# A two-layer hybrid decoder on one core: weights laid out by transfer, per-feature parameters laid out as columns

## The chip, the cores and the metric

The kernel runs on one core of a Trainium2 chip (trn2). The metric is device time in microseconds (us) of one execution. The kernel before takes 655.65 us, the median of three runs that lie between 655.14 and 657.24 us. Engines are named as the profile names them: PE is TensorE (PEld its weight loads), DVE is VectorE, ACT is ScalarE, POOL is GpSimd, and SP is the engine that issues most transfers.

## What is computed

The reference is a decoder trunk of two layers over 256 tokens of width 1024, all in float32:

```
for i in range(2):
    h   = rmsnorm(x, norm1_g[i])
    mix = hybrid_mixer(h, w_in[i], cmp_pos[i], cmp_w1[i], cmp_w2[i])     # 16 heads of three kinds
    x   = x + mix @ w_out[i]
    h   = rmsnorm(x, norm2_g[i])
    x   = x + conv_glu_ffn(h, w_up[i], conv_w[i], conv_b[i], w_down[i])  # 2 x 2816 wide, conv of 3 taps
return rmsnorm(x, final_g)
```

The input projection `h @ w_in` has 2615 columns: queries, keys and values of all heads. One kind of head (NSA) also attends to compressed blocks: blocks of 32 tokens of keys and of values get `cmp_pos` added, go through `cmp_w1` (2048 to 128), a GELU and `cmp_w2`. Two kinds of parameter thus enter: large weight matrices (w_in, cmp_w1, w_out, w_up, w_down), and per-feature vectors (the norm gains, conv_w, conv_b, cmp_pos), which multiply or shift one feature for all tokens.

## The kernel before, in words

**Weights.** Every weight tile but `cmp_w1` comes through `weight` (L148): SP issues one transfer from the weight as the caller gave it into a staging tile `st` (five buffers), ACT rounds it to the PE's fast float format into `hl` (L158), and DVE subtracts to get the rounding error (L160), so that each product is made of three matmuls (`mm3`, L207 to L210) with a high and a low part. `hl` has eight buffers, and a buffer comes free when the matmuls that read it are done. A `w_in` tile is two blocks of 128 rows by 336 to 384 columns (L163), so the transfer has two runs of 1.3 to 1.5 KB for each partition; a `w_up` tile has four runs of 1 KB per partition (L909), a `w_out` tile two runs of 2 KB (L803), a `w_down` tile one run of 4 KB (L911). The `cmp_w1` tile (L605) takes a buffer of `hl`, is used as it lands, and has 16 runs of 512 B per partition.

**Parameters.** The engines need a per-feature vector as a column: feature on the partition. Before, each vector is loaded as rows of 128 features (`rows_n`, and three parts of `rows`), turned by a PE transpose, and copied from PSUM to SBUF by DVE; `columns` (L139 to L142) does both steps. There are five such calls: norm1_g first of all (L232), cmp_pos ahead of the compressed heads (L591, into `colp`), and norm2_g with conv_b and the two layers' conv_w in the dilated heads of layer 0 (L820 to L822). The rows of the last four come by six transfers that POOL issues after the first norm (L270 and L126 to L131), among them `w2` (L271) and the mask constants `cb` (L127).

**Order.** Per layer: seven column chunks of `w_in` (`project`, L564 to L569; here A with 384 columns, B with 336, C with 360, then D to G with 384 each), four `st` transfers a chunk, as a generator that yields between groups of matmuls; `fill` interleaves these with the attention of the heads. After chunks A, B and most of C come the compressed heads: DVE copies the turned keys and values into `u2` (L547), adds the position column and makes `raw` (L597), and 64 small matmuls multiply by `cmp_w1` (L609). Then attention, the output projection (`out_part`) and the MLP, 11 blocks of 256 features: `up` and `down`. The order of instructions on each engine is fixed before the run by the framework's planner, which works with its own estimates of durations and may move an instruction ahead of others; `after(...)` pins a few of them behind a named one.

Of the kernel before, what the change touches and what calls it, by code (L numbers as in the profile page):

```python
# [12 lines left out]
F32 = mybir.dt.float32  # L13
# [7 lines left out]
D = 1024  # L21
DEPTH = 2
DFF = 2816
# [10 lines left out]
B_CAUS, B_DIL = 0, 256  # L34
CONSTB_W = B_DIL + 6 * 128
# [35 lines left out]
def trunk(ctx, tc, x, norm1_g, w_in, cmp_pos, cmp_w1, cmp_w2, w_out, norm2_g, w_up, conv_w, conv_b, w_down,  # L71
          final_g, eye, consts_f, consts_b, out):
# [25 lines left out]
    rn = keep.tile([16, 128], F32, name="rows_n")  # L98
# [3 lines left out]
    nc.scalar.dma_start(rn, norm1_g.rearrange("l (f p) -> (l f) p", p=128))  # L102
# [20 lines left out]
    rows = keep.tile([128, 512], F32, name="rows", tag="R", bufs=1)  # L123
    ra, rp_, rc = rows[:60, 0:128], rows[:64, 128:256], [rows[:66, 256 + 128 * i:384 + 128 * i] for i in range(DEPTH)]

    def other_constants():  # L126
        nc.gpsimd.dma_start(cb, consts_b)  # L127
        for a, b, src in ((0, 16, norm2_g), (16, 60, conv_b)):
            nc.gpsimd.dma_start(ra[a:b, :], src.rearrange("l (f p) -> (l f) p", p=128))
        for i in range(DEPTH):  # L130
            nc.gpsimd.dma_start(rc[i], conv_w[i].rearrange("w (f p) -> (w f) p", p=128))  # L131

    cola = keep.tile([128, 76], F32, name="cola")
    colp = keep.tile([128, DEPTH, 2, 16], F32, name="colp")
    colc = keep.tile([128, DEPTH, 66], F32, name="colc")
    gain1 = [cola[:, 8 * i:8 * i + 8] for i in range(DEPTH)]
    gain2 = [cola[:, 16 + 8 * i:24 + 8 * i] for i in range(DEPTH)]
# [74 lines left out]
    for i in range(DEPTH):  # L212

        with ExitStack() as es:
# [9 lines left out]
            if i == 0:  # L224
# [7 lines left out]
                columns(bank("t"), cola[:, 0:16], rn)  # L232

# [29 lines left out]
            def scales():  # L263
# [551 lines left out]


            dense.append(out_part((0, 1), (2, 3), (4,)))
# [56 lines left out]
            dense.append(out_part((5, 6), (7,)))  # L874
# [23 lines left out]
        with ExitStack() as es:  # L898
# [5 lines left out]
            wu = w_up[i].rearrange("(k p) c -> p k c", p=128)  # L904
            hs = {}

            def up(f):
                f0 = f * 256
                wh = [weight(wu[:, 4 * h:4 * h + 4, au * DFF + f0:au * DFF + f0 + 256], 4, 256)  # L909
                      for au in range(2) for h in range(2)]  # L910
                wd = [weight(w_down[i, (2 * f + s) * 128:(2 * f + s + 1) * 128, None, :], 1, 1024) for s in range(2)]  # L911
# [23 lines left out]
                for s in range(2):  # L935
                    cw = [colc[:, i, w * 22 + 2 * f + s:w * 22 + 2 * f + s + 1] for w in range(3)]
                    cw.append(cola[:, 32 + 22 * i + 2 * f + s:33 + 22 * i + 2 * f + s])
# [84 lines left out]
_INS = ['x', 'norm1_g', 'w_in', 'cmp_pos', 'cmp_w1', 'cmp_w2', 'w_out', 'norm2_g', 'w_up', 'conv_w', 'conv_b',  # L1022
        'w_down', 'final_g']
# [19 lines left out]
```

## Time and profile before

| | |
|---|---|
| median of 3 runs | 655.65 us (655.14 to 657.24) |
| the profiled execution | 657.55 us, its span 655.7 us |
| mean granted PE clock | 0.994 |
| PE busy | 636.8 us (97%) |
| DVE, ACT, POOL busy | 532.2, 400.0, 50.0 us |
| transfers | 76532 packets, 107.28 MB, mean 164 GB/s |

The span runs from the first to the last instruction; the execution has 1.85 us around it. Matmuls overlap, so that one of them is longer than the distance between two starts, and "busy" means that at least one is running. "[2.02 <-issue]" behind an instruction says that its engine was idle for 2.02 us before it and what ended the idle time; "issue" is used where the profile names no releaser. The DMA share is the mean busy share of the 16 DMA engines; it can come out a little above 1.

### The profile page before, as it was taken

The numbers are of one execution on the slowest core, as the hardware profiler recorded it, in microseconds if no ns is written. First come the engines' busy times: TensorE is split into PE (matmuls) and PEld (weight loads), VectorE is DVE, ScalarE is ACT, GpSimd is POOL, SyncE is SP. The second block draws the span as 40 slices with busy tenths as digits, with TensorE's granted clock in tenths as the row PEclk, the third lists the DMA queues.
The fourth block names the chain that finished last, engine by engine and source line by source line (L and its number), as shares of the span: only waits on it lengthen the run. The fifth ranks groups of instructions, "written<-read, shape, count | busy, mean of one in ns | idle before, by whom it ended". The sixth has DMA issues, their size and how long they took to land.

```text
span 655.7 us, 10521 instructions
## 1 busy us (share of the span) xinstructions
PE 636.8 (97%) x3699; PEld 543.2 (83%) x3699; DVE 532.2 (81%) x1185; ACT 400.0 (61%) x773; POOL 50.0 (8%) x119
## 2 busy tenths in 40 slices
PE   8989999999999999999999999999999999999995
PEld 7978987768888888888898888867788888888884
DVE  5879998776988888888777799987598888888873
ACT  6656776866655555555475676786675555555533
POOL 0422210001000000000020132000000000000002
PEclk9989999999999999999999999999999999999998
DMA  8983234453676666665457525234457666666501
GB/s 269 273 255 95 81 97 146 129 165 118 184 217 189 191 190 191 193 192 169 131 164 229 145 81 177 61 117 146 144 161 226 192 193 192 193 193 192 192 2 64
DMA packets 76532, 107.28 MB, mean 164 GB/s; under 512 B 3717, under 2 KB 63414, under 8 KB 76480
## 3 DMA queue, kind: packets, MB, share of 16 engines
q1 hardware_dynamic: 75568, 104.77, 52.9%
q0 software_dynamic: 448, 1.05, 0.5%
q10 hardware_dynamic: 464, 0.79, 0.3%
q8 instruction: 29, 0.48, 0.3%
q14 instruction: 23, 0.19, 0.1%
HBM read 105.55 MB, written 1.05 MB: 163 GB/s over the span
## 4 chain that ended last, share of the span: by engine, by line
PE 81%; DVE 11%; ACT 3%; issue 2%; DMA 1%; POOL 1%; SPq 0%; POOLq 0%; ACTq 0%; DVEq 0%
PE bu L924 24%; PE bu L926 13%; PE bn L208 6%; PE bn L209 6%; PE bn L210 6%; PE bd L208 5%; PE bd L209 5%; PE bd L210 5%; DVE hl L160 3%; PE bs L354 2%; PE bt L374 2%; PE bt L343 1%; DVE acc L486 1%; ACT hl L158 1%; PE bo L609 1%
## 5 line engine op out<-in xcount | busy, mean ns | idle before, releaser
L160 DVE TENSOR_TENSOR hl<-st,hl 128x1024 fp32r<-128x1024 f32 (+3 forms) x208 | 232.5, 1121 | 60.7 <-ACT hl L158 59.7
L158 ACT CAST hl<-st 128x1024 fp32r<-128x1024 f32 (+3 forms) x208 | 201.5, 972 | 121.7 <-PE bn L210 43.5
L924 PE MATMUL bu<-ahl,hl 128*128 128x512 f32 x704 | 177.9, 393 | 2.0 <-DVE ahl L196 2.0
L924 PEld LDWEIGHTS bu<-ahl,hl 128*128 128x128 f32 x704 | 127.2, 189 | 25.9 <-DVE ahl L196 2.8
L926 PEld LDWEIGHTS bu<-ahl,hl 128*128 128x128 f32 x704 | 96.7, 190 | 7.2
L926 PE MATMUL bu<-ahl,hl 128*128 128x256 f32 x704 | 99.3, 282 | 0.0
L208 PE MATMUL bd<-hl,ahl 128*128 128x384 f32 (+2 forms) x256 | 92.9, 367 | 0.9 <-DVE xr L813 0.5
L209 PE MATMUL bd<-hl,ahl 128*128 128x384 f32 (+2 forms) x256 | 91.2, 356 | 0.2 <-DVE hl L160 0.2
L210 PE MATMUL bd<-hl,ahl 128*128 128x384 f32 (+2 forms) x256 | 91.3, 357 | 0.0
L208 PE MATMUL bn<-hl,h_hi 128*128 128x512 f32 x176 | 69.0, 392 | 0.1
L209 PE MATMUL bn<-hl,h_hi 128*128 128x512 f32 x176 | 68.8, 391 | 0.0
L210 PE MATMUL bn<-hl,h_lo 128*128 128x512 f32 x176 | 68.5, 389 | 0.0
L929 ACT COPY cross<-bu 128x256 f32<-128x256 f32 x88 | 32.4, 369 | 40.0 <-PE bu L926 39.7
L208 PEld LDWEIGHTS bd<-hl,ahl 128*128 128x128 f32 x256 | 48.2, 189 | 9.8 <-issue 2.2
L209 PEld LDWEIGHTS bd<-hl,ahl 128*128 128x128 f32 x256 | 48.2, 188 | 3.4 <-issue 0.8
L210 PEld LDWEIGHTS bd<-hl,ahl 128*128 128x128 f32 x256 | 48.2, 188 | 3.0 <-issue 0.9
L941 DVE SCALAR_TENSOR_TENSOR c<-a,colc,c 128x255 f32<-128x255 f32 (+1 forms) x88 | 40.1, 482 | 7.5 <-ACT c L939 6.2
L210 PEld LDWEIGHTS bn<-hl,h_lo 128*128 128x128 f32 x176 | 33.0, 188 | 7.3 <-DVE h_lo L954 0.3
L208 PEld LDWEIGHTS bn<-hl,h_hi 128*128 128x128 f32 x176 | 33.1, 188 | 7.1 <-ACT h_hi L953 0.9
L209 PEld LDWEIGHTS bn<-hl,h_hi 128*128 128x128 f32 x176 | 33.1, 188 | 6.0
L939 ACT ACTIVATE c<-a,cola,colc 128x256 f32<-128x256 f32 x44 | 24.1, 595 | 13.5 <-DVE a L933 13.5
L930 DVE TENSOR_TENSOR sa<-bu,cross 128x256 f32<-128x256 f32 x44 | 18.4, 418 | 6.5 <-ACT cross L929 4.4
(243 smaller groups left out, 797.0 us busy)
## 6 DMA issues: line engine op xcount, KB each, us to landing
st<-in_w_up_dram SPq DMA_DIRECT2D x88, 512.0 KB, 4.1
st<-in_w_down_dram SPq DMA_DIRECT2D x44, 512.0 KB, 4.2
st<-in_w_in_dram SPq DMA_DIRECT2D x40, 384.0 KB, 3.9
st<-in_w_out_dram SPq DMA_DIRECT2D x12, 512.0 KB, 3.8
st<-in_w_in_dram SPq DMA_DIRECT2D x8, 360.0 KB, 3.2
st<-in_w_in_dram SPq DMA_DIRECT2D x8, 336.0 KB, 3.4
st<-in_w_out_dram SPq DMA_DIRECT2D x8, 256.0 KB, 2.9
xr<-in_x_dram SPq DMA_DIRECT2D x3, 256.0 KB, 5.2
```

What stands on the lines that cost most here:

```text
L158: S.copy(hv, sv)
L160: V.tensor_sub(lv, sv, hv.bitcast(F32))
L208: PE.matmul(b, ahi, whi, start=first, stop=False)
L209: PE.matmul(b, ahi, wlo, start=False, stop=False)
L210: return PE.matmul(b, alo, whi, start=False, stop=last)
L354: PE.matmul(b[:, o:o + nk], qa, ka, start=True, stop=True)
L924: PE.matmul(o, wa, hhl[k // 4][:, k % 4].rearrange("p z t -> p (z t)"), start=k == 0, stop=False)
L926: PE.matmul(o[:, :L], wl, hhi[k // 4][:, k % 4, :], start=False, stop=k == 7)
L929: S.copy(cross, o[:, L:])
L930: V.tensor_tensor(sums[au][:, s], o[:, :L], cross, op=OP.add)
L939: S.activation(c[:, o:o + 256], a[:, o:o + 256], AF.Identity, bias=cw[3], scale=cw[2])
L941: V.scalar_tensor_tensor(c[:, o + d:o + 256], a[:, o:o + 256 - d], cw[w], c[:, o + d:o + 256], op0=OP.mult, op1=OP.add)
```

## The change

All of it is in how the host hands over the inputs and how they are loaded. `laid_out` rearranges the weights on the host so that each `st` tile, and each `cmp_w1` tile, is one contiguous block with one run per partition (2.6 to 3 KB for `w_in`, 4 KB for `w_up` and the two-row groups of `w_out`, 8 KB for `cmp_w1`); `w_down` was one run before and stays. The number of transfers of weights, their sizes in bytes and their order in the program stay. The gains of norm1 come as a [128, 16] array, loaded by ACT straight into `cola`; all the other vectors come as one [128, 256] array, which POOL loads into `cols` by one transfer. The five transposes and the five copies are gone, and so are the tile `rows` and five of POOL's transfers.

```diff
+PIECES = ((0, 384), (384, 336), (1103, 360), (719, 384), (1463, 384), (1847, 384), (2231, 384))
+W_IN = {c: sum(n for _, n in PIECES[:j]) for j, (c, n) in enumerate(PIECES)}
+GROUPS = ((0, 1), (2, 3), (4,), (5, 6), (7,))
...
-    rn = keep.tile([16, 128], F32, name="rows_n")
+    cola = keep.tile([128, 16], F32, name="cola")
...
-    nc.scalar.dma_start(rn, norm1_g.rearrange("l (f p) -> (l f) p", p=128))
+    nc.scalar.dma_start(cola, gains)
...
-    def other_constants():
-        nc.gpsimd.dma_start(cb, consts_b)
-        for a, b, src in ((0, 16, norm2_g), (16, 60, conv_b)):
-            nc.gpsimd.dma_start(ra[a:b, :], src.rearrange("l (f p) -> (l f) p", p=128))
-        for i in range(DEPTH):
-            nc.gpsimd.dma_start(rc[i], conv_w[i].rearrange("w (f p) -> (w f) p", p=128))
...
+    cols = keep.tile([128, PARAMS_W], F32, name="cols")
...
-    def columns(b, dst, src):
-        n = src.shape[0]
-        PE.transpose(b[:, :n], src, ident[:n, :n])
-        V.tensor_copy(dst, b[:, :n])
+    gain2 = [cols[:, P_N2 + 8 * i:P_N2 + 8 * i + 8] for i in range(DEPTH)]
+    colp = cols[:, P_POS:P_POS + 64].rearrange("p (l c j) -> p l c j", l=DEPTH, c=2)
...
-        nc.sync.dma_start(sv, src)
+        nc.sync.dma_start(st[:, :a * n], src)
...
+    def piece(w, o, p, n):
+
+        return w[o:o + p * n].rearrange("(p n) -> p n", n=n)
+
     def w_in_chunk(i, c0, n, then=(None,) * 4, behind=(None, None)):
-        w = w_in[i].rearrange("(k p) c -> p k c", p=128)
-        return [weight(w[:, 2 * h:2 * h + 2, c0:c0 + n], 2, n, then[h], behind) for h in range(4)]
+        w = piece(w_in[i], W_IN[c0] * D, 4 * 128, 2 * n)
+        return [weight(w[h * 128:(h + 1) * 128], 2, n, then[h], behind) for h in range(4)]
...
-                columns(bank("t"), cola[:, 0:16], rn)
...
-                        nc.gpsimd.dma_start(rp_, cmp_pos.rearrange("l c (j p) d -> (l c j) (p d)", p=2))
-                    nc.gpsimd.dma_start(w2, cmp_w2[i].rearrange("c h d -> h c d"))
+                        nc.gpsimd.dma_start(cols, params)
+                    nc.gpsimd.dma_start(w2, cmp_w2[i].rearrange("h (c d) -> h c d", c=2))
                     if i == 0:
-                        other_constants()
+                        nc.gpsimd.dma_start(cb, consts_b)
...
-                if i == 0:
-                    with after(newest[0].ins):
-                        columns(bank("t"), colp.rearrange("p l c j -> p (l c j)"), rp_)
...
-                    nc.sync.dma_start(w1, cmp_w1[i, c].rearrange("(j p) h -> p j h", p=128))
+                    nc.sync.dma_start(w1.rearrange("p j h -> p (j h)"), cmp_w1[i, c])
...
-                        wh, wl = weight(w_out[i, g[0] * 128:(g[-1] + 1) * 128, n * 512:(n + 1) * 512]
-                                        .rearrange("(k p) c -> p k c", p=128), len(g), 512)
+                        wh, wl = weight(piece(w_out[i], (8 * n + g[0]) * 128 * 512, 128, len(g) * 512), len(g), 512)
...
-            if i == 0:
-                with after(newest[0].ins):
-                    columns(bank("t"), cola[:, 16:76], ra)
-                    for l in range(DEPTH):
-                        columns(bank("t"), colc[:, l, :], rc[l])
...
-                wh = [weight(wu[:, 4 * h:4 * h + 4, au * DFF + f0:au * DFF + f0 + 256], 4, 256)
+                wh = [weight(w_up[i, f, au, h], 4, 256)
                       for au in range(2) for h in range(2)]
...
+def laid_out(a):
+
+    w = a["w_in"].reshape(DEPTH, 4, 2, 128, -1).transpose(0, 1, 3, 2, 4)
+    w_in = np.concatenate([w[..., c:c + n].reshape(DEPTH, -1) for c, n in PIECES], 1)
...
+    w_up = a["w_up"].reshape(DEPTH, 2, 4, 128, 2, DFF // 256, 256).transpose(0, 5, 4, 1, 3, 2, 6)
+    w1 = a["cmp_w1"].reshape(DEPTH, 2, 16, 128, 128).transpose(0, 1, 3, 2, 4)
...
+    columns = lambda z: z.reshape(-1, 128).T
+    gains = columns(a["norm1_g"])
+    params = np.concatenate([columns(a[z]) for z in ("norm2_g", "conv_b", "cmp_pos", "conv_w")], 1)
```

## Rows read from the trace of the kernel before

**Rows 1.** The page's shares of the chain that ended last, by engine.

```profile
PE 81%; DVE 11%; ACT 3%; issue 2%; DMA 1%; POOL 1%; SPq 0%; POOLq 0%; ACTq 0%; DVEq 0%
```

**Rows 2.** Busy time by stretch. Columns: the stretch, its length, busy us and number of instructions of PE, PEld, DVE, ACT and POOL, then the granted PE clock, the DMA share and GB/s.

```profile
20.00:30.00 10.00, 9.19 (x64) 8.70 (x63) 8.11 (x22) 7.01 (x15) 5.12 (x10) 1.00 1.01 309
30.00:40.00 10.00, 8.14 (x51) 7.50 (x49) 8.32 (x28) 5.24 (x11) 0.26 (x1) 1.00 0.99 306
60.00:70.00 10.00, 9.86 (x54) 8.23 (x53) 9.89 (x45) 7.19 (x19) 2.19 (x7) 1.00 0.15 40
170.00:320.00 150.00, 150.00 (x798) 129.52 (x797) 122.21 (x177) 84.69 (x126) 0.00 (x0) 1.00 0.63 188
```

**Rows 3.** What ACT's weight casts waited for, over the whole span (total us, times, longest).

```profile
ACT hl L158 <- DMA st<-in_w_in_dram: 3.8, 4, 2.4
```

**Rows 4.** The first microseconds, instruction by instruction (start, duration, engine, line).

```profile
1.17 0.45 ACTq L102 DMA_DIRECT2D rows_n<-in_norm_g_dram  x1
5.28 0.26 PE L141 MATMUL bt<-ident,rows_n 16*128 16x16 f32 x1 [0.65 <-DMA ident<-in_eye_dram]
6.62 0.47 ACT L195 ACTIVATE ahl<-bt,cola 128x256 fp32r<-128x256 f32 x1 [3.47 <-PE bt L189]
```

**Rows 5.** Transfers by their issuing line: count, KB each, median us from issue to landing.

```profile
rows_n<-in_norm_g_dram ACTq DMA_DIRECT2D x1, 8.0 KB, 3.9
rows<-in_cmp_pos_dram POOLq DMA_DIRECT2D x1, 32.0 KB, 5.9
st<-in_w_up_dram SPq DMA_DIRECT2D x88, 512.0 KB, 4.1
st<-in_w_down_dram SPq DMA_DIRECT2D x44, 512.0 KB, 4.2
```

**Rows 6.** The chain that ended last, around 25 us (start, duration, what), and PE's row at the end of it.

```profile
18.85 5.51 DMA st<-in_w_in_dram
24.44 0.80 ACT hl L158
...
25.64 0.57 DVE qrT L523
...
26.26 0.55 PE L343 MATMUL bt<-ident,PA 128*128 128x128 f32 x3 [0.81 <-DVE qrT L523]
```

**Rows 7.** ACT, DVE and PE ahead of the compressed heads of layer 0.

```profile
36.29 0.84 ACT L158 CAST hl<-st 128x768 fp32r<-128x768 f32 x1 [2.40 <-DMA st<-in_w_in_dram]
...
34.79 0.92 DVE L547 COPY u<-bt 64x64 f32<-64x64 f32 x4
37.16 0.96 DVE L160 TENSOR_TENSOR hl<-st,hl 128x768 fp32r<-128x768 f32 x1 [1.45 <-ACT hl L158]
38.15 0.22 DVE L142 COPY colp<-bt 128x64 f32<-128x64 f32 x1
38.29 0.95 DVE L160 TENSOR_TENSOR hl<-st,hl 128x768 fp32r<-128x768 f32 x1
...
39.49 1.09 DVE L597 TENSOR_TENSOR raw<-u,colp 128x240 f32<-128x240 f32 x2
...
40.16 3.60 PE L609 MATMUL bo<-w,raw 128*32 128x128 f32 x64 [2.02 <-issue]
```

**Rows 8.** POOL's first issue of the parameters, SP's issues of the two `cmp_w1` tiles of layer 0 and of the `w_in` tile behind them, and all packets that moved in two stretches of 4 us, 30 to 34 and 34 to 38.

```profile
20.66 0.79 POOL L270 DMA_DIRECT2D rows<-in_cmp_pos_dram  x1
...
21.13 0.82 SPq L605 DMA_DIRECT2D w<-in_cmp_w_dram  x1
23.29 3.62 SPq L605 DMA_DIRECT2D w<-in_cmp_w_dram  x1
27.01 4.35 SPq L154 DMA_DIRECT2D st<-in_w_in_dram  x1
...
DMA packets 634, 1.18 MB, mean 295 GB/s; under 512 B 25, under 2 KB 159, under 8 KB 634
DMA packets 1019, 1.48 MB, mean 369 GB/s; under 512 B 59, under 2 KB 1014, under 8 KB 1019
```

**Rows 9.** The second half of the compressed-head matmuls of layer 1 (chain row: start, duration; the first half is in rows 10, and the 64 of layer 0 in rows 7), and the stretches of those of layer 0 and of the first half of layer 1 (columns as in rows 2).

```profile
361.42 1.01 PE bo L609 x32
...
40.20:43.70 3.50, 3.50 (x65) 3.16 (x65) 2.42 (x5) 0.83 (x1) 1.59 (x4) 0.52 0.79 234
358.50:359.60 1.10, 1.10 (x33) 0.90 (x33) 1.07 (x3) 0.00 (x0) 0.00 (x0) 1.00 0.59 221
```

**Rows 10.** The same place in layer 1: DVE's order and PE's wait.

```profile
356.84 0.94 DVE L547 COPY u<-bt 64x64 f32<-64x64 f32 x4
357.81 1.08 DVE L597 TENSOR_TENSOR raw<-u,colp 128x240 f32<-128x240 f32 x2
...
358.50 1.08 PE L609 MATMUL bo<-w,raw 128*32 128x128 f32 x32 [0.58 <-issue]
```

**Rows 11.** The transposes of the parameters that stand on the chain in layer 0 (cmp_pos; then norm2_g with conv_b, and conv_w twice).

```profile
35.28 0.20 PE bt L141
113.75 0.20 PE bt L141
114.73 0.06 PE bt L141
115.49 0.21 PE bt L141
```

More of the change, by code (lines that the diff above doesn't have):

```diff
@@ L34 @@
 B_CAUS, B_DIL = 0, 256
+P_N2, P_CB, P_POS, P_CW = 0, 16, 60, 124
+PARAMS_W = P_CW + 132
+PIECES = ((0, 384), (384, 336), (1103, 360), (719, 384), (1463, 384), (1847, 384), (2231, 384))
+W_IN = {c: sum(n for _, n in PIECES[:j]) for j, (c, n) in enumerate(PIECES)}
+GROUPS = ((0, 1), (2, 3), (4,), (5, 6), (7,))
 CONSTB_W = B_DIL + 6 * 128
@@ L70, in trunk @@
 @with_exitstack
-def trunk(ctx, tc, x, norm1_g, w_in, cmp_pos, cmp_w1, cmp_w2, w_out, norm2_g, w_up, conv_w, conv_b, w_down,
-          final_g, eye, consts_f, consts_b, out):
+def trunk(ctx, tc, x, w_in, cmp_w1, cmp_w2, w_out, w_up, w_down, final_g, gains, params, eye, consts_f, consts_b, out):
     nc = tc.nc
@@ L120, in trunk @@
     V.memset(neghalf, -0.5)
-    rows = keep.tile([128, 512], F32, name="rows", tag="R", bufs=1)
-    ra, rp_, rc = rows[:60, 0:128], rows[:64, 128:256], [rows[:66, 256 + 128 * i:384 + 128 * i] for i in range(DEPTH)]
-    def other_constants():
-        nc.gpsimd.dma_start(cb, consts_b)
-        for a, b, src in ((0, 16, norm2_g), (16, 60, conv_b)):
-            nc.gpsimd.dma_start(ra[a:b, :], src.rearrange("l (f p) -> (l f) p", p=128))
-        for i in range(DEPTH):
-            nc.gpsimd.dma_start(rc[i], conv_w[i].rearrange("w (f p) -> (w f) p", p=128))
-    cola = keep.tile([128, 76], F32, name="cola")
-    colp = keep.tile([128, DEPTH, 2, 16], F32, name="colp")
-    colc = keep.tile([128, DEPTH, 66], F32, name="colc")
-    gain1 = [cola[:, 8 * i:8 * i + 8] for i in range(DEPTH)]
-    gain2 = [cola[:, 16 + 8 * i:24 + 8 * i] for i in range(DEPTH)]
-    def columns(b, dst, src):
-        n = src.shape[0]
-        PE.transpose(b[:, :n], src, ident[:n, :n])
-        V.tensor_copy(dst, b[:, :n])
+    cols = keep.tile([128, PARAMS_W], F32, name="cols")
+    gain1 = [cola[:, 8 * i:8 * i + 8] for i in range(DEPTH)]
+    gain2 = [cols[:, P_N2 + 8 * i:P_N2 + 8 * i + 8] for i in range(DEPTH)]
+    colp = cols[:, P_POS:P_POS + 64].rearrange("p (l c j) -> p l c j", l=DEPTH, c=2)
     def after(ins):
@@ L814, in out_part @@
                 yield
-            dense.append(out_part((0, 1), (2, 3), (4,)))
-            if i == 0:
-                with after(newest[0].ins):
-                    columns(bank("t"), cola[:, 16:76], ra)
-                    for l in range(DEPTH):
-                        columns(bank("t"), colc[:, l, :], rc[l])
+            dense.append(out_part(*GROUPS[:3]))
             nm = pj.tile([128, 12], F32, name="nmd")
@@ L873, in trunk @@
             fill()
-            dense.append(out_part((5, 6), (7,)))
+            dense.append(out_part(*GROUPS[3:]))
             fill(3)
@@ L903, in trunk @@
             NF = DFF // 256
-            wu = w_up[i].rearrange("(k p) c -> p k c", p=128)
             hs = {}
             def up(f):
-                f0 = f * 256
-                wh = [weight(wu[:, 4 * h:4 * h + 4, au * DFF + f0:au * DFF + f0 + 256], 4, 256)
+                wh = [weight(w_up[i, f, au, h], 4, 256)
                       for au in range(2) for h in range(2)]
-                wd = [weight(w_down[i, (2 * f + s) * 128:(2 * f + s + 1) * 128, None, :], 1, 1024) for s in range(2)]
+                wd = [weight(w_down[i, (2 * f + s) * 128:(2 * f + s + 1) * 128, :], 1, 1024) for s in range(2)]
                 order = [(au, s, range(8)) for au in range(2) for s in range(2)]
@@ L935, in up @@
                 for s in range(2):
-                    cw = [colc[:, i, w * 22 + 2 * f + s:w * 22 + 2 * f + s + 1] for w in range(3)]
-                    cw.append(cola[:, 32 + 22 * i + 2 * f + s:33 + 22 * i + 2 * f + s])
+                    cw = [cols[:, o + 2 * f + s:o + 2 * f + s + 1]
+                          for o in [P_CW + 66 * i + 22 * w for w in range(3)] + [P_CB + 22 * i]]
                     o = s * 256
@@ L1019, in trunk @@
                 nc.scalar.dma_start(out[0, t * 128:(t + 1) * 128, 512:1024], y[1])
-_INS = ['x', 'norm1_g', 'w_in', 'cmp_pos', 'cmp_w1', 'cmp_w2', 'w_out', 'norm2_g', 'w_up', 'conv_w', 'conv_b',
-        'w_down', 'final_g']
+def laid_out(a):
+    w = a["w_in"].reshape(DEPTH, 4, 2, 128, -1).transpose(0, 1, 3, 2, 4)
+    w_in = np.concatenate([w[..., c:c + n].reshape(DEPTH, -1) for c, n in PIECES], 1)
+    w = a["w_out"].reshape(DEPTH, 8, 128, 2, 512)
+    w_out = np.concatenate([w[:, g[0]:g[-1] + 1, :, n].transpose(0, 2, 1, 3).reshape(DEPTH, -1)
+                            for n in range(2) for g in GROUPS], 1)
+    w_up = a["w_up"].reshape(DEPTH, 2, 4, 128, 2, DFF // 256, 256).transpose(0, 5, 4, 1, 3, 2, 6)
+    w1 = a["cmp_w1"].reshape(DEPTH, 2, 16, 128, 128).transpose(0, 1, 3, 2, 4)
+    w2 = a["cmp_w2"].transpose(0, 2, 1, 3)
+    columns = lambda z: z.reshape(-1, 128).T
+    gains = columns(a["norm1_g"])
+    params = np.concatenate([columns(a[z]) for z in ("norm2_g", "conv_b", "cmp_pos", "conv_w")], 1)
+    return dict(x=a["x"], w_in=w_in, cmp_w1=w1.reshape(DEPTH, 2, 128, -1), cmp_w2=w2.reshape(DEPTH, 128, -1), w_out=w_out,
+                w_up=w_up.reshape(DEPTH, DFF // 256, 2, 2, 128, 1024), w_down=a["w_down"], final_g=a["final_g"],
+                gains=gains, params=params)
 def kernel(**inputs):
@@ L1032 @@
     eye, cf, cb = shape_constants()
-    given = [(n, np.ascontiguousarray(inputs[n])) for n in _INS] + [("eye", eye), ("consts_f", cf),
-                                                                           ("consts_b", cb)]
+    given = [(n, np.ascontiguousarray(a)) for n, a in laid_out(inputs).items()] + [
+        ("eye", eye), ("consts_f", cf), ("consts_b", cb)]
     for name, a in given:
```

## The prediction

> **What bounds the kernel now.** I read the page's chain first. PE holds 81% of it and transfers 1% [rows 1], so a change to transfers can only pay where the PE stands still or does extra work. The busy time by stretch comes next [rows 2]. In the long MLP stretch from 170 to 320 us PE is busy for all 150.00 us while the DMA share is 0.63, so nothing in that stretch waits for weights. Between 20 and 40 us it is the other way round: the DMA share is 1.01 and 0.99, at 309 and 306 GB/s, and PE lacks 0.81 and 1.86 us. The third view is what ACT's weight casts waited for: over the whole span they waited 3.8 us for transfers, four times, 2.4 us at the longest [rows 3]. So the transfers matter in the first 40 us of layer 0 and hardly elsewhere, and I follow the timeline there.
>
> The clearest place is the compressed heads of layer 0. PE stands for 2.02 us before their 64 matmuls, until 40.16 us. These need `raw`, which DVE writes from 39.49 us on (1.09 us for two, so the first is there at about 40.04). DVE was late because ahead of `raw` in its queue stood a weight subtract that had waited 1.45 us for a cast, and that cast had waited 2.40 us for a `w_in` transfer, up to 36.29; then the `colp` copy (38.15) and another subtract (38.29) [rows 7]. The transfer was late because SP's queue was full of `cmp_w1`: the two issues at 21.13 and 23.29 and the next `w_in` issue at 27.01 held SP for 0.82, 3.62 and 4.35 us, and from 30 to 34 us, when `cmp_w1` with its runs of 512 B still came in, the rate was 295 GB/s, against 369 from 34 to 38, when almost all packets were `w_in` runs of 1.5 KB (1014 of 1019 under 2 KB) [rows 8]. And the stop cost more than itself: the 64 matmuls ran at a granted clock of 0.52 and took 3.60 us; in layer 1, behind a wait of 0.58 us, the two halves took 1.08 and 1.01 us, the first at 1.00 [rows 7, 9, 10]. 0.52 is practically the lower of the two levels, 1.2 GHz.
>
> **The change part by part.**
>
> *The start.* The norm1 transpose held PE for 0.26 us, at 5.28, after the identity had landed, and the first transposes of x and ACT's first step at 6.62 came behind it [rows 4]. Without it this moves up by 0.26, if the gains are there at 6.36. As rows they were issued at 1.17 and landed 3.9 us later [rows 4, 5], at 5.07. As columns they are 128 runs of 64 B, for which the trace has no row: if they take the 5.9 us of the cmp_pos transfer [rows 5], they land at 7.07 and the step loses 0.45. I take the nearer row (same queue, same bytes): gain 0.26, between -0.45 and 0.26.
>
> *The stall at 25 us.* PE lacked 0.81 us because a `w_in` tile issued at 18.85 landed after 5.51 us and ACT and DVE steps stood behind its cast [rows 6]. Its runs go from 1.4 to 2.9 KB. Nearest are `w_up` and `w_down`: 1 KB and 4 KB runs of equal bytes land after 4.1 and 4.2 us [rows 5], so longer runs of this size gain little. Gain 0.2, between 0 and 0.81.
>
> *cmp_w1 in one run, cmp_pos without a turn.* The two tiles are 2.10 MB. At 295 GB/s they occupy the engines for 7.1 us, at 369 for 5.7 [rows 8]: what is queued behind them lands 1.4 us earlier, the tile cast at 36.29 at about 34.9. With DVE's order kept, `raw` starts near 39.49 - 1.4 - 0.15 for the missing copy, 37.9, and PE's wait falls to about 0.8 after its own earlier start. But the order need not stay. Before, `raw` had to follow the copy of a transpose; now its column comes from a transfer that takes the place of POOL's issue at 20.66, which landed 5.9 us later [rows 5, 8], nine us ahead of need. In layer 1, where the columns were there already, the planner put `raw` right behind the four copies to `u2`, and PE waited 0.58 [rows 10]. In layer 0 these copies end at 35.71 [rows 7], before PE wants `raw`. So I keep 0.3 us of the wait: gain 1.7, between 0 and 2.02. Next late is then the rope of the indexer keys after chunk C, which stands behind PE's own work and moves with it. The transpose of cmp_pos is 0.20 us of PE on the chain [rows 11]: gain 0.20.
>
> *The clock.* A wait of 0.81 us left it at 1.00 [rows 2, 6], 2.02 us did not. If the wait is under 0.8, the 64 matmuls take 1.08 + 1.01 instead of 3.60 us: gain 1.5, between 0 and 1.5.
>
> *The other transposes* of layer 0 hold 0.20 + 0.06 + 0.21 on the chain [rows 11]: gain 0.47. Their copies leave a DVE that is busy 9.89 of 10 us in the stretch from 60 to 70 [rows 2], which can only help.
>
> *Nothing* for `w_up`, `w_out` and the rest of `w_in`: PE is busy throughout and hides them; for that cover to go, the MLP's transfers would have to take 1/0.63, some 1.6 times as long, and `w_down`, which has the new layout already, lands as `w_up` does [rows 2, 5]. Nothing for POOL's five fewer issues: it has 0.26 us of work from 30 to 40 [rows 2]. Layer 1's compressed heads waited for DVE's copies, not for a transfer: 0, at most the 0.58 [rows 10].
>
> *Sum:* 0.26 + 0.2 + 1.7 + 0.20 + 1.5 + 0.47 = 4.33 us. The profiled execution (657.55, with 1.85 outside its span of 655.7) lies 1.9 above the median of the runs; the gain is in its first 120 us, and I take it off the median: 655.65 - 4.33 = 651.3.
>
> **A rule against it.** From 30 to 34 us the rows give 295 GB/s with runs of 512 B, and 369 behind it with 1.5 KB [rows 8]. The Trainium skill, "DMA: Bandwidth & Descriptors", section "Specifications", puts the smallest transfer that reaches line rate at 512 B; by that, no transfer here was slowed by its runs, and none gets faster. The two rates speak against it, though POOL's transfers shared part of the first stretch.
>
> **The rivals.**
>
> *Same rate, same order.* If run length does not matter and DVE keeps its order, the wait at 38 us and the low clock stay. What is left is 0.26 + 0.20 + 0.47: 654.7. This is also the case in which the transfers are cut into short pieces again. For it: 1 KB and 4 KB runs land alike [rows 5]. Against: the two rates [rows 8], and that `raw` is freed from the transpose in any case. 17%. (It is the case that the rule above would give.)
>
> *Half the wait, low clock.* The wait falls to 1.2 us or so and the clock falls all the same; the trace has no wait between 1 and 2 us that tells. Gain 0.26 + 0.2 + 0.8 + 0.20 + 0.47 = 1.9: 653.7. 10%.
>
> *A worse order: slower.* The planner orders by estimated durations, and the change alters its estimates for the weight transfers and takes five copies out. Rows 7 and 10 show that the same code got two orders in the two layers. DVE from 60 to 70 us has 0.11 us to spare [rows 2]; each weight subtract put ahead of the index loop there costs 0.95 us [rows 7] and PE waits with it. From the fifth one on the gain is eaten; one chunk of four in each layer is 7.6 us: 655.65 - 4.33 + 7.6 = 658.9. Against it: number, order and bytes of the transfers stay. 13%.
>
> **How the numbers follow.** The forecast has 60%. Its own range is 649.8 (all upper ends: 0.26 + 0.81 + 2.02 + 0.20 + 1.5 + 0.47 + 0.58 = 5.84) to 653; with all lower ends, -0.45 + 0.20 + 0.47, nothing is left of the gain. 0.3%, 2.0 us, is about what a measurement of this kernel can tell from no change: the line lies at 653.7. Faster: the 60% and half of the second rival, 65%. Same: the first rival and the other half, 22%. Slower: 13%. The range runs from 649.2 to 655.8, which takes in the first two rivals.
>
> **What would show it.** Right: no stop of 2 us before the 64 matmuls of layer 0, these in 2.1 us at a clock of 1.00, over 340 GB/s while `cmp_w1` comes in, PE's first transpose of x at about 5.2, and from 120 us on every instruction some 4 us earlier and otherwise alike. Wrong: a PE wait on ACT's first step at 6.4 (late gains), casts still waiting for transfers near 36 us, or DVE subtracts in new places between 60 and 110 with PE idle behind them.

## The result, and the profile after

The changed kernel takes 652.38 us (median of 4 runs, 651.78 to 653.55); the kernel before, on the same chip, 656.44 us (4 runs, 655.14 to 657.27). The ratio is 0.9938, 95% interval [0.9918, 0.9958]: 4.06 us faster. The forecast was 651.3 us with a gain of 4.33 us; the gain of 0.6% is beyond the 0.3% set as the bound. Run once more later, against 17 runs of before, the changed kernel gave 652.28 us and 0.9936 [0.9921, 0.9950].

The profiled execution of the changed kernel took 651.93 us (span 650.1, mean granted clock 0.997). The first trace of before is of an execution of 657.55 us, so this pair is 5.6 us apart, more than the medians; a second trace of each is used below to tell what belongs to the kernels.

The busy time by stretch, columns as in [rows 2]:

```profile
20.00:30.00 10.00, 10.00 (x71) 9.75 (x70) 9.25 (x27) 7.57 (x16) 2.23 (x5) 1.00 0.98 362
30.00:40.00 10.00, 8.98 (x107) 8.07 (x106) 9.55 (x27) 5.86 (x11) 1.32 (x3) 1.00 0.80 272
```

From 20 to 30 us the transfers now move 362 GB/s in place of 309 at the same DMA share, PE no longer stands, and by 40 us the share has fallen to 0.80: the transfers have caught up.

ACT, DVE and PE ahead of the compressed heads of layer 0, which answer to [rows 7]:

```profile
33.07 0.83 ACT L147 CAST hl<-st 128x768 fp32r<-128x768 f32 x1 [0.73 <-DMA st<-in_w_in_dram]
...
33.24 0.94 DVE L538 COPY u<-bt 64x64 f32<-64x64 f32 x4
34.20 1.08 DVE L585 TENSOR_TENSOR raw<-u,cols 128x240 f32<-128x240 f32 x2
...
34.89 1.08 PE L597 MATMUL bo<-w,raw 128*32 128x128 f32 x32 [1.01 <-issue]
...
37.91 1.08 PE L597 MATMUL bo<-w,raw 128*32 128x128 f32 x32
```

The cast waits 0.73 us in place of 2.40. `raw` stands right behind the copies to `u2`, as in layer 1 [rows 10]. The 64 matmuls come in two halves of 1.08 us. PE still stands 1.01 us before them.

SP's issues of the two `cmp_w1` tiles and of the next `w_in` tile, and all packets from 24 to 28 us, which answer to [rows 8]:

```profile
20.52 0.33 SPq L593 DMA_DIRECT2D w<-in_cmp_w_dram  x1
22.68 0.33 SPq L593 DMA_DIRECT2D w<-in_cmp_w_dram  x1
23.22 0.44 SPq L143 DMA_DIRECT2D st<-in_w_in_dram  x1
...
DMA packets 298, 1.57 MB, mean 393 GB/s; under 512 B 53, under 2 KB 53, under 8 KB 157
```

SP was held for 0.82, 3.62 and 4.35 us there; now for 0.33, 0.33 and 0.44. Transfers by line, as in [rows 5] (count, KB each, median us from issue to landing):

```profile
st<-in_w_up_dram SPq DMA_DIRECT2D x88, 512.0 KB, 4.0
...
cola<-in_gains_dram ACTq DMA_DIRECT2D x1, 8.0 KB, 4.4
```

The `w_up` tiles land after 4.0 us with one run of 4 KB per partition, after 4.1 with four of 1 KB.

The first microseconds, as in [rows 4]:

```profile
5.59 0.63 PE L182 MATMUL bt<-ident,xr 128*128 128x128 f32 x4 [0.95 <-DMA ident<-in_eye_dram]
...
6.25 0.47 ACT L188 ACTIVATE ahl<-bt,cola 128x256 fp32r<-128x256 f32 x1 [3.10 <-PE bt L182]
```

ACT's first step waits for PE alone: the gains were there.

To place the gain I use the starts of a few PE instructions as milestones: the first matmul of the projection, the first of chunk C, the first of the 64, the transposes of kd (the indexer's keys), the first of layer 0's MLP and of layer 1's. Each column is the time from the milestone of the column before it, worked out from PE's timeline of each trace (us; the two last rows are experiments that come below):

```
                       to first  ..C    ..the 64  ..kd   ..MLP 0  ..MLP 1  ..end of span
before, first trace     9.09    20.23   10.84    7.76   98.66   317.21   191.9
before, second trace    9.07    19.53   11.14    7.30   98.72   317.33   192.0
after, first trace      8.52    19.21    7.16    8.67   97.35   317.33   191.9
after, second trace     8.88    19.23    7.12    8.67   97.36   317.31   191.9
cmp_w1 alone            8.43    19.68    9.43    6.29   98.66   317.25   192.0
parameters alone        8.16    21.06    7.12    9.32   97.34   317.25   192.0
```

All of the gain is ahead of layer 0's MLP. Between the second traces (656.85 and 652.28 us) it is 0.19 at the start, 0.30 up to chunk C, 2.65 from there to kd (18.44 to 15.79), 1.36 from kd to the MLP, and 0.1 in the rest. One more thing differs that the description of the change doesn't name: `cmp_w2` (64 KB a layer) is also rearranged on the host, as the diff shows. Of the experiments only "`cmp_w1` alone" and those built on the kernel before lack that; no run parts it from the rest.

### The profile page after: what moved, and what is told of

It is laid out like the page before. It is cut to its first block, busy times and chain, and to the rows that moved or that the text cites. A ratio compares the mean times of both kernels' runs of the same rounds, so it can differ in the third digit from the quotient of the medians.

```text
span 650.1 us, 10491 instructions
## 1 busy us (share of the span) xinstructions
PE 631.1 (97%) x3694; PEld 538.3 (83%) x3694; DVE 531.6 (82%) x1180; ACT 399.3 (61%) x773; POOL 48.0 (7%) x115
## 3 DMA queue, kind: packets, MB, share of 16 engines
q0 software_dynamic: 336, 1.05, 0.4%
HBM read 105.55 MB, written 1.05 MB: 164 GB/s over the span
## 4 chain that ended last, share of the span: by engine, by line
PE 78%; DVE 14%; ACT 3%; issue 2%; POOL 1%; DMA 1%; POOLq 0%; SPq 0%; DVEq 0%; ACTq 0%
PE bu L904 24%; PE bu L906 13%; PE bn L201 6%; PE bn L202 6%; PE bn L203 6%; PE bd L201 5%; PE bd L203 4%; PE bd L202 4%; DVE hl L149 4%; PE bt L365 1%; PE bs L345 1%; DVE acc L477 1%; DVE P L753 1%; ACT hl L147 1%; DVE m L476 1%
## 5 line engine op out<-in xcount | busy, mean ns | idle before, releaser
L203 PE MATMUL bd<-hl,ahl 128*128 128x384 f32 (+2 forms) x256 | 91.5, 357 | 0.0
L203 PE MATMUL bn<-hl,h_lo 128*128 128x512 f32 x176 | 68.5, 389 | 0.0
L203 PEld LDWEIGHTS bd<-hl,ahl 128*128 128x128 f32 x256 | 48.2, 188 | 3.4 <-issue 1.2
L921 DVE SCALAR_TENSOR_TENSOR c<-a,cols,c 128x255 f32<-128x255 f32 (+1 forms) x88 | 40.0, 481 | 7.5 <-ACT c L919 6.3
L203 PEld LDWEIGHTS bn<-hl,h_lo 128*128 128x128 f32 x176 | 33.0, 188 | 7.3 <-DVE h_lo L934 0.3
L919 ACT ACTIVATE c<-a,cols 128x256 f32<-128x256 f32 x44 | 24.1, 595 | 13.5 <-DVE a L913 13.5
```

The source lines that it names most:

```text
L203: return PE.matmul(b, alo, whi, start=False, stop=last)
L919: S.activation(c[:, o:o + 256], a[:, o:o + 256], AF.Identity, bias=cw[3], scale=cw[2])
L921: V.scalar_tensor_tensor(c[:, o + d:o + 256], a[:, o:o + 256 - d], cw[w], c[:, o + d:o + 256], op0=OP.mult, op1=OP.add)
```

## The experiments

**The kernel before and the changed one, traced again.**

> The kernel before once more, for a second trace of it. The first trace is 0.9 us above the median of its runs, and from it alone one can't tell what of each wait is the layout's and what is that execution's. If the waits belong to the kernel, the 64 matmuls begin 21.1 us after the third group of the projection begins (21.12 in the first trace), behind a stop of 2 us or more and at the low clock, whatever the wait at 25 us is (0.81 in the first trace, 0 to 1.2 in the three kernels that add matmuls of zeros to it). If not, the stop is under 1 us or the clock full, and half of the forecast gain was that execution's.

> The changed kernel once more, on the same chip as the two others: 4.1 us below the kernel before, within 0.5 us; the wait before the copies of the second half of the queries (25 us) is anywhere between 0 and 1.5 us, by every theory.

Measured: before 656.42 us (11 runs) against 656.66 of the runs beside it, 0.9998 [0.9987, 1.0008]; after 652.28, 0.9936 [0.9921, 0.9950]. The second trace of before, PE from the 64 matmuls to kd, and two stretches (columns as in [rows 2]):

```profile
39.74 3.05 PE L609 MATMUL bo<-w,raw 128*32 128x128 f32 x64 [2.30 <-issue]
...
43.79 0.31 PE L617 MATMUL bo<-cf,hsum 128*128 128x16 f32 x2
...
47.04 0.44 PE L448 MATMUL bt<-ident,kd 128*128 128x128 f32 x2 [0.53 <-ACT kd L445]
...
39.74:40.40 0.66, 0.66 (x25) 0.66 (x29) 0.66 (x2) 0.00 (x0) 0.58 (x3) 1.00 0.99 326
40.45:43.75 3.30, 3.30 (x50) 2.92 (x40) 2.19 (x6) 1.66 (x2) 1.01 (x2) 0.50 0.79 210
```

In the second trace of the changed kernel, the first half of the 64 and kd:

```profile
35.23 1.08 PE L597 MATMUL bo<-w,raw 128*32 128x128 f32 x32 [0.95 <-issue]
...
43.90 0.44 PE L439 MATMUL bt<-ident,kd 128*128 128x128 f32 x2 [1.04 <-ACT kd L436]
```

The stop before the 64 (2.30 us, 2.02 in [rows 7]) and the low clock belong to the kernel. Where the low clock falls does not: here it began some 0.7 us after the 64 had begun, so that they took 3.05 us, not 3.60, and it lasted to 43.8, over the three matmuls of the projection behind them. From the first of the 64 to PE's next start behind these three it is 4.05 us (39.74 to 43.79), and 4.13 in the first trace.

The stall of 0.81 us at 25 us [rows 6] is not in this trace's waits at all, and yet the 64 begin only 0.43 us earlier, 20.69 us after chunk B's first matmul, against 21.12 with the stall; the stop before them is longer. By as much, 0.43 us, the `w_in` tile ahead of `raw` is cast earlier (35.86, 36.29 in [rows 7]). So the start of the 64 follows that transfer, and part of the stall is paid out of the later stop. That before would have gained little by losing the stall alone is argued from this; it was not run.

**Only cmp_w1 in one run; and all weights, but no columns.**

```diff
-                    nc.sync.dma_start(w1, cmp_w1[i, c].rearrange("(j p) h -> p j h", p=128))
+                    nc.sync.dma_start(w1.rearrange("p j h -> p (j h)"), cmp_w1[i, c])
```

> Only cmp_w1 in one run per partition, all else as before. My theory (of the weights, cmp_w1 is the one that holds up the queue): SP no longer stands at its issue, the w_in tile behind it lands 1.4 us earlier or more, the wait falls under 1 us and the clock stays; 2 to 3 us faster than before. Rival (the longer runs of w_in and the rest share the gain): the wait stays over 1.5 us, less than 1 us faster.

The other kernel has the changed kernel's weights, every one of them, and the rows and transposes of before:

```diff
-        w = w_in[i].rearrange("(k p) c -> p k c", p=128)
-        return [weight(w[:, 2 * h:2 * h + 2, c0:c0 + n], 2, n, then[h], behind) for h in range(4)]
+        w = piece(w_in[i], W_IN[c0] * D, 4 * 128, 2 * n)
+        return [weight(w[h * 128:(h + 1) * 128], 2, n, then[h], behind) for h in range(4)]
...
+                wh = [weight(w_up[i, f, au, h], 4, 256)
```

> All weights in one run per partition, the parameters as rows with their five transposes as before. My theory: raw still stands behind two weight subtracts and the colp copy, but the w_in transfer lands some 1.5 to 3 us earlier, the wait is 0.5 to 1 us and the clock stays at 1.00; 2.5 to 3.5 us faster than before. Rival (only the order of DVE matters): the wait stays near 2 us with the low clock, 0 to 0.7 us faster.

Measured: `cmp_w1` alone 653.88 us, 0.9965 [0.9953, 0.9976]; all weights 654.22 us, 0.9969 [0.9956, 0.9981]. In the second, PE's stop before the 64 is 0.65 us and the 64 take 1.95. The layout of `w_in`, `w_out` and `w_up` adds nothing to that of `cmp_w1`. The trace with `cmp_w1` alone (the cast; PE; all packets from 26 to 30 us):

```profile
33.48 0.83 ACT L158 CAST hl<-st 128x768 fp32r<-128x768 f32 x1 [0.79 <-DMA st<-in_w_in_dram]
...
37.54 1.95 PE L609 MATMUL bo<-w,raw 128*32 128x128 f32 x64 [0.59 <-issue]
...
40.02 0.29 PE L617 MATMUL bo<-cf,hsum 128*128 128x16 f32 x2
...
DMA packets 335, 1.56 MB, mean 389 GB/s; under 512 B 78, under 2 KB 109, under 8 KB 184
```

and the same two in the second trace of before (the cast; the packets from 26 to 30 us):

```profile
35.86 0.84 ACT L158 CAST hl<-st 128x768 fp32r<-128x768 f32 x1 [2.69 <-DMA st<-in_w_in_dram]
...
DMA packets 626, 1.19 MB, mean 298 GB/s; under 512 B 105, under 2 KB 138, under 8 KB 625
```

In the same stretch, with POOL's transfers as they were and the DMA share at 1.02 and 1.05, the rate is 389 GB/s in place of 298; the `w_in` tile is cast 2.38 us earlier, and DVE's `raw`, in its old place behind the copy to `colp`, begins at 36.86 in place of 39.07. PE's wait falls from 2.30 to 0.59 and the 64 take 1.95 us. With the three matmuls behind them it is 2.48 us (37.54 to 40.02), in the order of before, where it was 4.05 and 4.13: the low clock cost 1.6 us of PE's time in both traces of before. The way from chunk C to kd is 15.72 us, against 18.44. That is as short as in the changed kernel (15.79). The Trainium skill, "DMA: Bandwidth & Descriptors", section "Specifications", has the line rate from transfers of 512 B on; by that this kernel would have taken the time of the kernel before, 656.72 us beside it. It took 653.88, so the measurement decides against the rule here.

**Only the parameters as columns.**

```diff
-    rn = keep.tile([16, 128], F32, name="rows_n")
+    cola = keep.tile([128, 16], F32, name="cola")
...
-                if i == 0:
-                    with after(newest[0].ins):
-                        columns(bank("t"), colp.rearrange("p l c j -> p (l c j)"), rp_)
...
-                    columns(bank("t"), cola[:, 16:76], ra)
-                    for l in range(DEPTH):
-                        columns(bank("t"), colc[:, l, :], rc[l])
```

> The parameters as columns, all weights strided as before. My theory (the wait before the 64 compressed-head matmuls has two causes, each enough by itself to bring it under 1 us): DVE puts raw right behind the copies to u2, PE waits under 1 us there, the matmuls take 2.1 us at a clock of 1.00, the rate while cmp_w1 comes in stays near 295 GB/s; 3 to 4 us faster than before. Rival (the transfers alone do it): the wait of 2 us and the clock of 0.5 stay and only the transposes are saved, 0.5 to 1 us faster.

Measured: 653.6 us, 0.9955 [0.9941, 0.9968]. The cast for DMA, then PE:

```profile
36.03 0.83 ACT L147 CAST hl<-st 128x768 fp32r<-128x768 f32 x1 [2.24 <-DMA st<-in_w_in_dram]
...
36.34 1.08 PE L597 MATMUL bo<-w,raw 128*32 128x128 f32 x32 [1.00 <-issue]
...
45.66 0.44 PE L439 MATMUL bt<-ident,kd 128*128 128x128 f32 x2 [1.22 <-ACT kd L436]
```

The `w_in` tile is as late as before (36.03), and the stop of 2 us with its low clock is gone all the same: `raw` no longer stands behind that tile's subtract. But the late transfers show up elsewhere. In this trace PE waits 1.5 us at 25 us, and from the first matmul to kd it takes 37.50 us, only 0.5 less than in the second trace of before (37.97). Another 0.9 us of this trace's lead lies at the start (8.16 and 9.07), most of it from what the last section tells and not from the columns. What the columns give for certain is the stretch behind kd: 97.34 us in place of 98.7.

**cmp_w1 and the columns, the other weights as before.**

```diff
-        w = piece(w_in[i], W_IN[c0] * D, 4 * 128, 2 * n)
-        return [weight(w[h * 128:(h + 1) * 128], 2, n, then[h], behind) for h in range(4)]
+        w = w_in[i].rearrange("(k p) c -> p k c", p=128)
+        return [weight(w[:, 2 * h:2 * h + 2, c0:c0 + n], 2, n, then[h], behind) for h in range(4)]
...
-                        wh, wl = weight(piece(w_out[i], (8 * n + g[0]) * 128 * 512, 128, len(g) * 512), len(g), 512)
...
-                wh = [weight(w_up[i, f, au, h], 4, 256)
```

> The changed kernel with w_in, w_out and w_up as in the kernel before; only cmp_w1 lies in one run per partition, and the parameters are columns. The theory that of the weights only cmp_w1's layout counts: the time is that of the changed kernel, within 0.5 us (about 4 us below the kernel before). Rival, one run for w_in, w_out or w_up pays a part that is hidden when it is alone: the time is 1 us or more above the changed kernel.

Measured: 651.81 us, 0.9935 [0.9921, 0.9949], the time of the changed kernel. Two parts of the change carry all of its gain.

**Three transposes put back.**

```diff
+            if i == 0:
+                with after(newest[0].ins):
+                    for n in (60, 66, 66):
+                        b = bank("t")
+                        PE.transpose(b[:, :n], ident[:n, :], ident[:n, :n])
```

> The changed kernel, with three fp32 transposes of the first rows of the identity (60, 66 and 66 of them) put back in layer 0 where the transposes of the parameter rows stood; their results are not read and not copied. The theory that the columns save PE's time and the change between kinds of matmul around it, 1.31 us between kd's transposes and the MLP: the changed kernel's time and about 1.3 us. Rival, the transposes themselves are worth the 0.47 us that was predicted for them, and the rest of the 1.31 us came from the copies or from the DMA of the rows: the changed kernel's time and about 0.5 us. Within 0.2 us of the changed kernel, the price was wholly elsewhere.

Measured: 653.5 us, 0.9958 [0.9946, 0.9969], 1.7 us above the kernel of the last experiment, which ran beside it, and 1.1 to 1.2 above the changed kernel's medians. Its trace, 98.28 us from kd to the MLP in place of 97.3:

```profile
109.05 0.27 PE L809 MATMUL bt<-ident 60*128 60x60 f32 x1
109.25 0.50 PE L201 MATMUL bd<-hl,ahl 128*128 128x512 f32 x1
109.59 0.22 PE L809 MATMUL bt<-ident 66*128 66x66 f32 x1
109.61 0.48 PE L202 MATMUL bd<-hl,ahl 128*128 128x512 f32 x1
110.03 1.31 PE L389 MATMUL bo<-T,vv 128*64 128x256 f32 x10
111.27 0.28 PE L809 MATMUL bt<-ident 66*128 66x66 f32 x1
111.47 0.93 PE L345 MATMUL bs<-kdT,qdT 64*128 64x128 f32 x8
...
120.23 0.50 PE L201 MATMUL bd<-hl,ahl 128*128 128x512 f32 x1 [0.80 <-DVE xr L800]
```

and the same matmuls in the changed kernel:

```profile
108.35 0.48 PE L201 MATMUL bd<-hl,ahl 128*128 128x512 f32 x1
108.66 0.39 PE L202 MATMUL bd<-hl,ahl 128*128 128x512 f32 x1
108.89 0.40 PE L203 MATMUL bd<-hl,ahl 128*128 128x512 f32 x1
109.22 1.31 PE L389 MATMUL bo<-T,vv 128*64 128x256 f32 x10
110.46 0.93 PE L345 MATMUL bs<-kdT,qdT 64*128 64x128 f32 x8
```

With the transposes, two matmuls of a product and the ten of L389 take 2.42 us (109.05 to 111.47). In the changed kernel the same work is 0.31 + 0.23 + 1.24 = 1.78 us, so that the three cost 0.64 in this place, 0.21 each. The product's third matmul (L203), which followed at 0.23 us before the next start, is parted from the others and now stands alone behind L345. Over the whole stretch from kd to the MLP it is 0.95 us for the three, a good two thirds of the 1.3; there PE's later waits differ too (0.80 us for `xr`, which neither kernel has, and 0.52 ahead of the MLP in place of 0.99). What makes up the rest the kernels with zeros show. These three, the next experiment, keep the transposes and the copies, but set the 64 in two halves with projection between them, as the changed kernel does. They take 98.32 to 98.37 us from kd to the MLP: 1.0 more than the changed kernel, and 0.35 less than before. So about 1.0 of the 1.31 to 1.36 us comes with the transposes and their copies, and about 0.35 with the order around the 64; how that acts behind kd was not taken apart.

**Zeros against the low clock.** Matmuls of zeros in the kernel before, ahead of the 64, in three forms: eight in a bank of the transposes, eight in an unused half of the bank of the 64, and 28 there. The first form and the third (the second is the third with eight):

```diff
+                    if i == 0 and c == 0:
+                        with after(newest[0].ins):
+                            b = bank("t")
+                            for j in range(8):
+                                PE.matmul(b[:, :256], zero[:, 0:128], zero, start=j == 0, stop=j == 7)
```

```diff
+                    if i == 0 and c == 0:
+                        with after(newest[0].ins):
+                            for j in range(28):
+                                PE.matmul(hb[:, 256:512], zero[:, 0:128], zero, start=j == 0, stop=j == 27)
```

> The kernel before, with eight matmuls of zeros in PE's wait of 2 us ahead of the compressed-head matmuls of layer 0 (1.8 us of PE that stood still). My theory (the stop lowers the granted clock and this costs 1.5 us): the 64 matmuls start when they did, run at a clock of 1.00 in 2.1 us instead of 3.6, and the kernel is 1 to 1.5 us faster. Rival (the clock costs nothing, since what follows waits for the rope of the indexer keys on POOL): the same time or slower by up to 0.3 us.

> The kernel before, with eight matmuls of zeros (256 columns each) into the unused half of the PSUM bank that the 64 matmuls of the compressed heads write, in layer 0 and the first pair of heads, where the engine stands before them; nothing of the output changes. The theory that the stop makes the clock low and that this costs about 1.5 us: the 64 matmuls begin no later than in the kernel before, all at the full clock, some 2.0 us for both halves in place of 3.6 (rows 7, 9), and the time is 1.0 to 1.5 us below the kernel before. Rival, the low clock costs nothing because something else ends at the same time: the matmuls are at the full clock and the time is within 0.5 us of the kernel before. If the 64 still run at 1.2 GHz, the run says nothing.

> The kernel before with 28 matmuls of zeros in layer 0, in place of the eight of the run before, which were put ahead of the last group of the projection and so left a stop of 2.90 us. 28 of them take some 2.8 to 3.0 us, so the group behind them ends about 1 us before VectorE has written raw. The theory that the stop makes the clock low and that the low clock costs about 1.5 us by itself: the 64 matmuls begin where they began (near 39.5), 1.08 us for each 32 at the full clock in place of 1.93, and the time is 1.0 to 1.5 us below the kernel before. Rival, other engines end at the same time whatever the clock: the 64 are at the full clock and the time is within 0.5 us of the kernel before.

Measured: 657.63 us, 1.0017 [1.0007, 1.0028]; 657.34 us, 1.0017 [1.0005, 1.0028]; 658.32 us, 1.0026 [1.0015, 1.0037]. All three are slower, by 0.2 to 0.3%. The first form waited 2.38 us for the bank, ahead of the zeros; the granted clock fell 1.2 us behind that stop, and the first half of the 64 took 1.94 us. In the second form the zeros ran too early:

```profile
34.08 1.05 PE L610 MATMUL bo<-zero 128*128 128x256 bf16 x8
...
39.51 1.93 PE L613 MATMUL bo<-w,raw 128*32 128x128 f32 x32 [2.90 <-issue]
```

The third form has a stop of 1.42 us and the full clock:

```profile
36.27 3.23 PE L610 MATMUL bo<-zero 128*128 128x256 bf16 x28
40.92 1.08 PE L613 MATMUL bo<-w,raw 128*32 128x128 f32 x32 [1.42 <-issue]
```

The 64 begin as late after chunk C as before (10.76 us), now at 1.08 us a half, but 12 matmuls of the projection that had filled the time ahead of them now stand between the halves. The order changed with the clock, so these runs can't price the low clock by itself. What they and the others do show is when it came: behind stops of 0.59, 1.01 and 1.42 us the 64 ran at a granted clock of 1.00 (2.4 GHz); with stops of 2.02, 2.30, 2.38 and 2.90 us it fell to 0.50 (1.2 GHz), between 0.1 us before PE's next start and 1.2 us after it. The length of the last stop alone does not decide it, as the next experiment shows.

**Two tries at the wait that is left.** One group of the projection more ahead of the compressed heads (`AHEAD` 6), and `raw` of the first pair written ahead of the last copies for the second.

```diff
-AHEAD = 5
+AHEAD = 6
```

```diff
+                        if t:
+                            raw(c)
...
-                raw2 = []
-                for c in range(2):
-                    r = pj.tile([128, 17, 16], F32, name=f"raw{c}", tag=f"raw{c}")
```

> The changed kernel with one more group of the input projection set ahead of the compressed heads' matmuls (AHEAD 6 for 5), so that TensorE has work while VectorE writes raw. The theory that the 1.01 us which TensorE still stands before the 64 matmuls is for want of work in that place: the wait is gone in layer 0, and the time is up to 1.0 us below the changed kernel, 0.6 in layer 1 besides. Rival, the group set ahead needs its own weights or bank sooner and waits for those, or raw's own copies move back with it: no gain, within 0.5 us of the changed kernel or above it.

> The changed kernel with VectorE's addition for the first head pair (raw0) put right behind the two copies of u that it reads, ahead of the two copies for the second pair, in both layers. The theory that the 1.01 us before the 64 matmuls is VectorE's four copies and first addition, and that what comes later hangs on TensorE's groups: raw0 is written some 0.47 us (two copies) earlier, the wait falls to about 0.5 us in layer 0 and to about 0.1 in layer 1, and the time is 0.5 to 1.0 us below the changed kernel. Rival, the next wait (1.04 us for ScalarE's kd) takes it up: the wait before the 64 is shorter, the one before kd longer by as much, and the time is that of the changed kernel.

Measured: 657.17 us, 1.0005 [0.9993, 1.0016], and 652.0 us, 0.9937 [0.9918, 0.9956]. With `AHEAD` 6 PE's wait before the 64 is 0.19 us, as hoped, and kd comes 0.9 us earlier, but behind a longer wait:

```profile
35.09 1.08 PE L597 MATMUL bo<-w,raw 128*32 128x128 f32 x32 [0.19 <-issue]
...
42.86 0.44 PE L439 MATMUL bt<-ident,kd 128*128 128x128 f32 x2 [1.59 <-ACT kd L436]
```

From kd to the MLP it then takes 99.48 us (97.35 in the changed kernel), and from MLP to MLP 320.10 (317.3): 4.9 us are lost for 0.9. In layer 1 the trace shows where a good part of it goes:

```profile
361.40 0.44 PE L439 MATMUL bt<-ident,kd 128*128 128x128 f32 x2 [1.54 <-ACT kd L436]
...
362.40:365.60 3.20, 3.20 (x12) 3.20 (x11) 3.00 (x8) 1.53 (x4) 0.00 (x0) 0.50 0.41 125
```

PE waits 1.54 us for kd there (0.71 in the changed kernel), and 0.9 us later the granted clock falls to 0.50, up to 365.7, and in this stretch the matmuls of the projection begin 0.32 us apart in place of 0.17. Behind the 1.59 us in layer 0 it stayed at 1.00. The 2.1 us that layer 0 loses behind kd were not taken apart; that the group moved ahead is missing in other holes is an argument.

With `raw` first, the planner put three of the four copies ahead of it, not two:

```profile
33.42 0.69 DVE L549 COPY u<-bt 64x64 f32<-64x64 f32 x3
34.04 0.57 DVE L529 TENSOR_TENSOR raw<-u,cols 128x240 f32<-128x240 f32 x1
...
34.71 0.54 PE L600 MATMUL bo<-w,raw 128*32 128x128 f32 x12 [0.77 <-issue]
```

The wait falls by 0.2 us, and the time can't be told from the changed kernel's 652.28 beside it. Neither is a version that beats both kernels.

## Why the prediction was right

The sign, the place and nearly the size came out: 4.33 us forecast, 4.06 measured, and 4.57 between the second traces. That the size came so near is in part luck: two terms were off by 0.8 to 0.9 us each, in opposite directions. The time itself was 1.1 us low, and most of that is the base: the sum was taken off the 655.65 us of three runs, and before has since given medians of 656.4 to 656.9. The lower end of the stated range, 649.2, doesn't follow from the working either, whose upper ends add up to 649.8. Term by term, against the second traces:

*The start, 0.26: right.* 0.19 us between them (9.07 and 8.88); PE's first transpose of x begins at 5.29, and at 5.59 in the first trace, where it waited 0.95 us for the identity. The gains land 4.4 us after their issue, near the 3.9 chosen, and nothing waits for them. Between the first traces it is 0.57, of which most has another cause (last section).

*The stall at 25 us, 0.2: right in size, wrong in its cause.* Up to chunk C the second traces differ by 0.30. But the stall varies with the execution (0.81, none, and 0 to 1.2 us in three kernels with the old layout), and in before part of it was paid out of the later stop. The layout of `w_in`, to which the term was put down, does nothing: without it the time is the same. The traces point to `cmp_w1`, which shares the queue: where it lies in one run the wait is 0.2 us at most (eight traces), and where it does not, up to 1.5 (six traces).

*The wait, cmp_pos and the clock, 1.7 + 0.2 + 1.5: the mechanism right, the wait too large.* It is 2.65 us between the second traces. `cmp_w1` at a better rate, an earlier `w_in` tile, no stop above 2 us and the 64 at 1.00 all came as said, and so did the two independent causes: either alone ends the stop and the low clock. The clock was priced nearly rightly at 1.5: it cost 1.6 us of PE's time in either trace of before. What fell short is the wait. The residual was set at 0.3 us and is 0.95 and 1.01, and the next wait, for kd, which was to move with PE's work, grew from 0.53 to 1.04 in the second traces (0.92 to 1.04 in the first). So PE's two waits between chunk C and kd shrank by 0.84 us together (2.83 to 1.99), not by 1.7. With the clock's 1.6 and the 0.2 of the transpose that gives the 2.65. The residual was worked out with PE's order kept, and the order changed: PE has done the work ahead of the 64 at 33.88 us in place of 38.14 [rows 7], 6.15 us behind the start of chunk C in place of 8.82, because 17 matmuls of that chunk now stand behind the first half, 11 of them between the halves as 10 do in layer 1, in place of 3.

*The other transposes, 0.47: too small.* The stretch from kd to the MLP shortened by 1.31 to 1.36 us, about 1.0 of it for the transposes and about 0.35 for the order around the 64, to which the forecast gave nothing. The step took the shares on the chain [rows 11], 0.06 us for one of them. A share on the chain counts the transpose until PE's next start and not what it does to the matmul behind it: in place the three cost 0.64. This error and the last one, of opposite sign, nearly cancel.

*Nothing for w_up, w_out, the rest of w_in, POOL's issues and layer 1: right.* From the first MLP to the second it is 317.1 to 317.4 us in every trace, `AHEAD` 6 apart; in layer 1 the order and the wait are those of [rows 10]:

```profile
351.21 0.94 DVE L538 COPY u<-bt 64x64 f32<-64x64 f32 x4
352.18 1.08 DVE L585 TENSOR_TENSOR raw<-u,cols 128x240 f32<-128x240 f32 x2
...
352.86 1.08 PE L597 MATMUL bo<-w,raw 128*32 128x128 f32 x32 [0.59 <-issue]
```

*The rivals.* "Same rate, same order" fell on both: 298 to 389 GB/s by the layout of `cmp_w1` alone, and `raw` freed by the columns alone. "Half the wait, low clock" fell because the wait of 1.0 us left the clock at 1.00; `AHEAD` 6, with the fall behind 1.54 us, shows how near it was. "A worse order" did not happen here, but `AHEAD` 6 shows that it is no idle fear: with one group moved the time was 657.17 us against 651.81 of the kernel with `cmp_w1` and the columns, which ran beside it.

What stays open: how much of the gain the two causes share. Alone they give 3.0 [2.1, 3.9] and 2.3 us [1.6, 3.1], together 4.1, so that about 1.2 us are counted twice, with an uncertainty as large as that.

## What to carry to other kernels

Where several stalls wait for one queue of transfers, they may be one stall: price the last of them, and look where the wait goes when its place is mended (the columns alone moved it to 25 us and to kd). A small instruction that splits a run of matmuls can cost more than its share of the chain, here 0.64 us in place, and 0.95 over the stretch, for three that the chain puts at 0.47. A low clock is priced over everything that runs at it: here it began and ended at other instructions in the second trace, and cost the same. And before a wait is priced from one trace, a second trace of the same kernel tells which part of it is the execution's.

## What was unexpected in the hardware

PE's first microseconds have two speeds that the printed clock does not tell. The eight matmuls of zeros ahead of the first projection took 1.04 us in the changed kernel's first trace and 1.91 in its second, and the granted clock of the stretch from 5 to 9 us is printed as 1.00 in both.

```profile
6.49 1.04 PE L222 MATMUL bd<-zero 128*128 128x256 bf16 x8
```

```profile
7.03 1.91 PE L222 MATMUL bd<-zero 128*128 128x256 bf16 x8
```

Of the 14 traces of all these kernels five have the long form, both of the kernel before among them. From the first transpose of x to the first matmul of the projection it costs 0.7 us (3.6 against 2.9). That is larger than the term that was forecast for the start, and it comes and goes with the execution.

The other surprise is SP: one issue of a 1 MB transfer of 2048 runs held it for 3.62 us [rows 8], and 2.60 in the second trace, where the other of the pair held it for 0.82 and 0.83; with 128 runs of 8 KB each held it for 0.33.
